# Two weight blocks a group get their low part by an accumulating DMA

## The chip, the cores and the metric

The kernel runs on one core of a Trainium2 chip. The metric is the device time of one execution in microseconds. The core has a matrix engine (TensorE, "PE" in the profile, with its weight loads as "PEld"), VectorE (DVE), ScalarE (ACT), GpSimd (POOL) and SyncE (SP). SP, ACT and POOL can issue DMAs; POOL's go to another queue than SP's.

## What is computed

A trunk of two layers over one sequence of 256 tokens with 2048 features, all in float32: a Conformer convolution layer, then an attention layer, each followed by a gated feed-forward part. The change lies in the two feed-forward parts:

```python
def _swiglu(h, w_gate, w_up, w_down):
    return (jax.nn.silu(h @ w_gate) * (h @ w_up)) @ w_down

h = h + _swiglu(_rmsnorm(h, ffn_norm_g[layer]), ffn_w_gate[layer], ffn_w_up[layer], ffn_w_down[layer])
```

`w_gate` and `w_up` are 2048 x 5632, `w_down` is 5632 x 2048; there is a set of them for each layer.

## The kernel before

**High and low parts.** A product of float32 operands is made from rounded parts (the type F32R). Each operand is split: the high part is the rounded value, the low part is the value less the high part. For a weight block, ACT writes the high part `whi` by a copy that rounds (line 242), and DVE writes the low part `wlo` by a subtraction, raw minus high (line 244). PE then makes three products: activation-high with `whi` (line 420), activation-low with `whi` (line 421), activation-high with `wlo` (line 424). In these products the activation is the operand that PE loads as weights (PEld) and the block of the weight matrix is streamed.

**Blocks.** A weight block is 128 partitions x 1024 float32, 512 KB. SP loads it from DRAM into one of three `raw` buffers (line 294). `whi` and `wlo` have four buffers each. `emit_block` writes out the load and the split of the next block in the list `blocks`; `next_block` sees to it that two blocks beyond the one that PE uses have been written out. A buffer is taken again once its last reader is done: a `raw` buffer after the subtraction that reads it, a `whi` or `wlo` buffer after PE's products with it. `in_order` keeps the splits in their order on ACT and on DVE. Apart from that, a scheduler orders each engine's instructions when the program is built.

**Groups.** Gate and up matrices are worked through in 11 groups of 512 columns for each of the two feed-forward parts (`ffn_hidden`, line 918). Group 0 uses 16 plain blocks. The ten later groups follow the pattern `ITEMS_FF = "nnSnSnSn"`: each `n` stands for one gate block and one up block, and each `S` for a product of 2 x 2 parts that is made with seven multiplications in place of eight. Its sums and differences of weight blocks are made by DVE in `emit_sums` (line 253) from two blocks that POOL loads in `load_sums` (lines 232 and 233); each `S` is four entries in the list. So a later group has 22 entries: ten plain blocks and three `S`. Written as positions, the plain ones are 0 to 3 (two gate blocks, then two up blocks), 8 and 9, 14 and 15, 20 and 21; the `S` entries are 4 to 7, 10 to 13 and 16 to 19. PE uses the entries in this order. Groups alternate between two sets of result banks, called `pp` and `aux`/`b`, for their plain products.

**Between groups.** When a group's products are complete, `combine` and `hidden` (lines 888 to 903) join them, apply SiLU on ACT and multiply on DVE. A few steps into the next group `turned` (line 905) transposes the result on PE, and ACT (line 915) and DVE (line 916) split it into the high and low part of `hid`. This last step frees banks that the first `S` of that group uses.

**The list is made ahead** in `plan_two`, which is called once for each group of gate and up, and for the two halves of `w_down`, with `n_rest` 0 for the former and 3 for the latter:

```python
        ahead = [next(plain) for _ in range(2)]
        blocks.extend((*w, k, GKV) for w in ab for k in ahead)
```

Of the kernel before, what the change touches and what calls it, by code (L numbers as in the profile page):

```python
# [10 lines left out]
F32R = mybir.dt.float32r  # L11
AF = mybir.ActivationFunctionType
ALU = mybir.AluOpType
# [5 lines left out]
S = 256  # L19
# [26 lines left out]


SUMS_FF = 3
LATE = 4
ITEMS_FF = "nnSnSnSn"  # L50

# [41 lines left out]
def trunk(ctx: ExitStack, tc: tile.TileContext, xT, vec, const, w1, w2, wk, wv, wq, wo, wg0, wu0, wd0, wg1, wu1, wd1, fing, out):  # L93
    nc = tc.nc
# [52 lines left out]
    def new_x(pool, name, n=DT):  # L147

        return pool.tile([P, n, 2, S], F32R, name=name)
# [8 lines left out]

    blocks = []
    all_sums = []  # L160

    def plan(w, u, kt_n, gk=GK):
        blocks.extend((w, u, g, gk) for g in range(kt_n // gk))
# [4 lines left out]
    def pairs_of(items, n_sums):  # L168

        n = n_sums if "S" in items else 0  # L170
        return iter(range(n)), iter(range(n, len(items)))

    def plan_two(a, b, items, n_sums, n_rest):

        sums, plain = pairs_of(items, n_sums)
        ab = a, b
        assert items.startswith("nn") and "S" not in items[len(items) - n_rest:]
        ahead = [next(plain) for _ in range(2)]
        blocks.extend((*w, k, GKV) for w in ab for k in ahead)
        for item in items[2:len(items) - n_rest]:  # L180
            if item == "S":
                k = next(sums)
                blocks.extend(("sums", len(all_sums), q, GKV) for q in range(4))
                all_sums.append((a, b, k))
            else:
                k = next(plain)
                blocks.extend((*w, k, GKV) for w in ab)
        rest = list(plain)
        assert len(rest) == n_rest and next(sums, None) is None
        blocks.extend((*w, k, GKV) for w in ab for k in rest)  # L190
# [29 lines left out]
    @contextmanager  # L220
    def in_order(eng):

        with tc.issue_after(last_split[eng]) if eng in last_split else nullcontext():
            made = []
            yield made
        last_split[eng] = made[-1].ins

    def load_sums(n):

        a, b, k = all_sums[n]  # L230
        src = [w[c, k].rearrange("p (k n) -> p k n", k=GKV) for w, c in (a, b)]
        nc.gpsimd.dma_start(places[0][:, 0:4:3, :], src[0])
        nc.gpsimd.dma_start(places[0][:, 1:3, :], src[1])  # L233
# [6 lines left out]
    def split(hi, lo, raw):  # L240
        with in_order("ACT") as made:
            made.append(nc.scalar.copy(hi, raw))  # L242
        with in_order("DVE") as made:
            made.append(nc.vector.tensor_tensor(out=lo, in0=raw, in1=hi.bitcast(F32), op=ALU.subtract))  # L244

    def emit_sums(n, q, _):

        hi, lo = (wp.tile([P, GKV, NBV], F32R, name=n, bufs=AHEAD + 2) for n in ("whi", "wlo"))
        four, t13, t24 = places

        def less(o, a, b):
            with in_order("DVE") as made:
                made.append(nc.vector.tensor_tensor(out=o, in0=a, in1=b, op=ALU.subtract))  # L253

        if q == 0:
            split(hi, lo, four[:, 0:4:3, :])
            less(t13, four[:, 1:3, :], four[:, 0:2, :])
        elif q == 1:
            split(hi[:, 1, :], lo[:, 1, :], four[:, 2, :])
            less(t24[:, 0, :], four[:, 2, :], t13[:, 0, :])  # L260
            less(t24[:, 1, :], four[:, 3, :], t24[:, 0, :])
        elif q == 2:
            split(hi, lo, t13)
        else:
            split(hi, lo, t24)
            if n + 1 < len(all_sums) and all_sums[n + 1][0][0] is all_sums[n][0][0]:
                load_sums(n + 1)
        ready.append((None, hi, lo))

    def emit_block():  # L270
        i = len(ready)
        if blocks[i][0] == "sums":
            emit_sums(*blocks[i][1:])
            return
        w, u, g, gk = blocks[i]
        natural = any(w is a for a in (wg0, wu0, wd0, wg1, wu1, wd1))
        shape = [P, gk, GK * NB // gk]
        native = NATIVE if g == 0 and (w is w1 or w is w2 and u < 2) else 0
        if native:
            raw = conv_pool[0].tile(shape, F32, name="rawn", bufs=2)  # L280
        else:
            raw = wp.tile(shape, F32, name="raw", bufs=RAW)
        hi = lo = None
        if native < gk:
            hi = wp.tile(shape, F32R, name="whi", bufs=AHEAD + 2)
            lo = wp.tile(shape, F32R, name="wlo", bufs=AHEAD + 2)
        src = w[u, g].rearrange("p (k n) -> p k n", k=gk)
        with_x = w is w1 and u == 0
        step = gk if not with_x else 1 if g == 0 else 2
        for s in range(0, gk, step):  # L290
            if with_x:
                load_x(GK * g + s, step)
            part = slice(s, s + step)
            nc.sync.dma_start(raw[:, part, :], src[:, part, :])
            part = slice(max(s, native), s + step)
            if natural:
                split(hi, lo, raw)
                continue
            if part.start < part.stop:
                nc.scalar.copy(hi[:, part, :], raw[:, part, :])  # L300
                eng = nc.gpsimd if (w is w1 and u > 1) or (w is w2 and u < 2 and (u, g) in ((0, 1), (1, 1), (0, 2))) else nc.vector
                eng.tensor_tensor(out=lo[:, part, :], in0=raw[:, part, :], in1=hi[:, part, :].bitcast(F32), op=ALU.subtract)  # L302
        ready.append((raw, hi, lo))
        if with_x and g == DT // GK - 1:
            x_loaded()
# [12 lines left out]
    def later(n, fn):  # L318
        queue.append([n, fn])
# [203 lines left out]
    with tc.tile_pool(name="cv", bufs=1) as cv, tc.tile_pool(name="cvu", bufs=1) as cvu:  # L523
# [11 lines left out]
        def load_x(kt, n):  # L535
            nc.sync.dma_start(hT[:, kt:kt + n, :], xT[:, kt:kt + n, :])
            for j in range(kt, kt + n):
                if j < NATIVE:
                    nc.vector.tensor_scalar(out=xf[:, j, :], in0=hT[:, j, :], scalar1=v("a_g", j), scalar2=None, op0=ALU.mult)
                else:  # L540
                    split_scaled(x, j, v("a_g", j))

        def x_loaded():
            nc.sync.dma_start(cst, const)
            nc.sync.dma_start(vecs[:, 3 * DT:], vec[:, 3 * DT:])
            for j in range(0, DT, 2):
                norm.add(hT[:, j:j + 2, :], *((nc.gpsimd, nc.gpsimd) if j < 4 else (nc.scalar, nc.vector)))
# [138 lines left out]
        for _ in range(3):  # L686
            emit_block()
# [77 lines left out]
    def sum_up(sums, u, two, h, d):  # L765

        h, d = h.rearrange("p (a b) -> p a b", b=S), wide(d)
        two = two.bitcast(F32)
        nc.vector.tensor_tensor(out=h, in0=two[:, :, 0, :], in1=two[:, :, 1, :], op=ALU.add)
        a11, a21, a12, a22 = (h[:, j, t * P:(t + 1) * P] for j in range(2) for t in range(2))  # L770
        for i, a, b, op in ((0, a21, a22, ALU.add), (1, d[:, 0, :], a11, ALU.subtract), (2, a11, a21, ALU.subtract),
                            (3, a12, d[:, 1, :], ALU.subtract)):
            nc.vector.tensor_tensor(out=d[:, i, :], in0=a, in1=b, op=op)
        nc.scalar.copy(sums[:, u, :, 0, :], d)
        nc.vector.tensor_tensor(out=sums[:, u, :, 1, :], in0=d, in1=sums[:, u, :, 0, :].bitcast(F32), op=ALU.subtract)
# [80 lines left out]
    def room(name):  # L856
        return sp.tile([P, 2, S], F32, name=name).rearrange("p a b -> p (a b)")
# [7 lines left out]
    def ffn_hidden(ff, scratch, wg, wu, x, norm):  # L865

        nonlocal hT
        hid = Joined()
        hid.add(new_x(ff, "hid", FT - LATE), FT - LATE)
        rooms = ff.tile([P, 2, 2, NBV], F32, name="rooms", tag="late")  # L870
        sums = ff.tile([P, SUMS_FF, 4, 2, P], F32R, name="xsums", tag="t8")
        later(2, lambda: norm.rstd_nat(bank2))
        for k in range(SUMS_FF):
            later(3 + 3 * k, lambda k=k: sum_up(sums, k, x[:, 2 * k:2 * k + 2, :, :], room("sq"), room("sq")))
# [30 lines left out]
        def turned(c, cs):  # L905

            if c == F // NBV - 1:
                hid.add(ff.tile([P, LATE, 2, S], F32R, name="hid2", tag="late"), LATE)
            for i in range(2):
# [8 lines left out]
        for c in range(F // NBV):  # L918
            items = ff_items(c)
            cs = (second_banks if c % 2 else first_banks)()  # L920
            two_blocks((wg, c), (wu, c), items, SUMS_FF, 0, x, sums, cs, first_banks if c % 2 else second_banks, combine)
            if c == 0:
# [59 lines left out]
    with tc.tile_pool(name="at", bufs=1) as ap:  # L982
# [46 lines left out]
        for c in range(D // NBV):  # L1029
            bk = project_nat(wv, c, x)  # L1030
            for t in range(2):
                nc.scalar.activation(vn[:, t, c * NBV:(c + 1) * NBV], bk[t], AF.Identity,
                                     scale=norm.rn[:, t:t + 1])
# [138 lines left out]
```

## Time and profile before

| | |
|---|---|
| median of 3 runs | 2133.26 us (2132.51 to 2134.04) |
| the profiled execution | 2134.19 us |
| its span, first to last instruction | 2132.4 us |
| clock granted to TensorE | 0.998 of full speed |
| bytes moved by DMA | 410.65 MB |

The span is what the profile's shares are taken of; the execution is 1.8 us longer. In the trace PE passes from one later gate and up group to the next in about 42.6 us; the ten groups lie between 366 and 793 us for the first layer and between 1460 and 1887 us for the second. A plain block is twelve products, which PE begins 0.23 us apart; the duration of one, 0.39 us, is longer since they are pipelined.

In the rows of groups, a line has the source line, the engine, the operation, the tile written and the tiles read, the shapes, the count, and then the busy time in us and the mean of one in ns, and the idle time ahead with what ended it. A row of DMA issues ends with the size of one and the median time in us from issue to landing. A row of waits has who waited for whom, the total in us, the number of times, and the longest. A row of the timeline begins with the start in us from the beginning of the span and the length.

### The profile page before, as it was taken

The numbers are of one execution on the slowest core, as the hardware profiler recorded it, in microseconds if no ns is written. First come the engines' busy times: TensorE is split into PE (matmuls) and PEld (weight loads), VectorE is DVE, ScalarE is ACT, GpSimd is POOL, SyncE is SP. The second block draws the span as 40 slices with busy tenths as digits, with TensorE's granted clock in tenths as the row PEclk, the third lists the DMA queues.
The fourth block names the chain that finished last, engine by engine and source line by source line (L and its number), as shares of the span: only waits on it lengthen the run. The fifth ranks groups of instructions, "written<-read, shape, count | busy, mean of one in ns | idle before, by whom it ended". The sixth has DMA issues, their size and how long they took to land.

```text
span 2132.4 us, 28640 instructions
## 1 busy us (share of the span) xinstructions
PE 2112.3 (99%) x10490; PEld 1789.5 (84%) x10490; DVE 1725.0 (81%) x2323; ACT 1172.0 (55%) x1525; POOL 344.1 (16%) x333
## 2 busy tenths in 40 slices
PE   9999899999999999999999999999999999999998
PEld 8999788888888888888888888888888888888886
DVE  6888876888998898878745677676899899988877
ACT  6665545555555555555644566555555555555454
POOL 5999110000000000000000100011000000000200
PEclk9999999999999999999999999999999999999999
DMA  7555357555655567565665644566556565566664
GB/s 246 185 159 169 97 182 244 177 189 198 213 189 190 199 201 243 192 195 194 193 192 183 189 152 148 174 201 213 198 197 201 194 200 195 198 221 217 210 213 150
DMA packets 114942, 410.65 MB, mean 193 GB/s; under 512 B 12912, under 2 KB 13936, under 8 KB 114800
## 3 DMA queue, kind: packets, MB, share of 16 engines
q1 hardware_dynamic: 87264, 310.21, 45.1%
q0 software_dynamic: 26816, 97.53, 13.1%
q8 instruction: 82, 1.34, 0.2%
q10 hardware_dynamic: 720, 1.07, 0.1%
q14 instruction: 60, 0.49, 0.1%
HBM read 402.47 MB, written 6.29 MB: 192 GB/s over the span
## 4 chain that ended last, share of the span: by engine, by line
PE 96%; DVE 1%; DMA 1%; ACT 0%; issue 0%; POOL 0%; SPq 0%; DVEq 0%; ACTq 0%; POOLq 0%
PE pp L420 12%; PE pp L424 12%; PE pp L421 12%; PE pp L346 10%; PE aux L420 9%; PE aux L424 9%; PE aux L421 9%; PE pp L388 7%; PE pp L350 5%; PE b L420 2%; PE b L421 2%; PE b L424 2%; PE pp L413 1%; DMA raw<-w 1%; PE pp L401 0%; DVE aux L587 0%
## 5 line engine op out<-in xcount | busy, mean ns | idle before, releaser
L244 DVE TENSOR_TENSOR wlo<-raw,whi 128x1024 fp32r<-128x1024 f32 x360 | 431.9, 1230 | 107.1 <-ACT whi L242 93.3
L242 ACT CAST whi<-raw 128x1024 fp32r<-128x1024 f32 x360 | 369.7, 1050 | 250.0 <-DMA raw<-wd 74.7
L300 ACT CAST whi<-raw 128x1024 fp32r<-128x1024 f32 (+1 forms) x209 | 216.1, 1037 | 231.1 <-PE pp L346 93.9
L302 DVE TENSOR_TENSOR wlo<-raw,whi 128x1024 fp32r<-128x1024 f32 (+1 forms) x164 | 201.9, 1243 | 137.8 <-ACT whi L300 116.5
L242 ACT CAST whi<-rooms 128x1024 fp32r<-128x1024 f32 x120 | 126.5, 1055 | 200.4 <-DVE rooms L253 174.2
L420 PE MATMUL pp<-whi,x 128*128 128x512 f32 x522 | 204.7, 392 | 0.0
L421 PE MATMUL pp<-whi,x 128*128 128x512 f32 x522 | 203.2, 389 | 0.0
L420 PE MATMUL aux<-whi,x 128*128 128x512 f32 x414 | 163.7, 395 | 0.0
L421 PE MATMUL aux<-whi,x 128*128 128x512 f32 x414 | 161.3, 390 | 0.0
L233 POOL DMA_DIRECT2D work<-wu x60 | 33.4, 556 | 748.4 <-DVE rooms L253 712.2
L244 DVE TENSOR_TENSOR wlo<-rooms,whi 128x1024 fp32r<-128x1024 f32 x120 | 146.6, 1222 | 8.7 <-ACT whi L242 5.3
L424 PE MATMUL pp<-wlo,x 128*128 128x512 f32 x522 | 150.6, 389 | 0.0
L244 DVE TENSOR_TENSOR wlo<-work,whi 128x1024 fp32r<-128x1024 f32 x120 | 114.4, 954 | 42.3 <-ACT whi L242 41.8
L587 DVE SCALAR_TENSOR_TENSOR aux<-up,vecs,aux 128x256 f32<-128x256 f32 x350 | 140.9, 481 | 1.5 <-ACT aux L585 1.5
L242 ACT CAST whi<-work 128x1024 fp32r<-128x1024 f32 x120 | 95.8, 833 | 77.2 <-DMA work<-wg 42.3
L424 PE MATMUL aux<-wlo,x 128*128 128x512 f32 x414 | 135.1, 390 | 0.0
L420 PE MATMUL pp<-whi,hid 128*128 128x512 f32 x306 | 119.2, 390 | 0.0
L421 PE MATMUL pp<-whi,hid 128*128 128x512 f32 x306 | 119.1, 389 | 0.0
L420 PEld LDWEIGHTS pp<-whi,x 128*128 128x128 f32 x522 | 98.0, 188 | 22.9 <-DVE hid L916 2.9
L424 PEld LDWEIGHTS pp<-wlo,x 128*128 128x128 f32 x522 | 98.0, 188 | 20.6
L421 PEld LDWEIGHTS pp<-whi,x 128*128 128x128 f32 x522 | 98.0, 188 | 20.0
L388 PE MATMUL pp<-x,whi 128*128 128x256 f32 x600 | 111.9, 288 | 0.0
(306 smaller groups left out, 4865.7 us busy)
## 6 DMA issues: line engine op xcount, KB each, us to landing
raw<-wd SPq DMA_DIRECT2D x128, 512.0 KB, 4.2
raw<-wg SPq DMA_DIRECT2D x116, 512.0 KB, 4.0
raw<-wu SPq DMA_DIRECT2D x116, 512.0 KB, 4.0
raw<-w SPq DMA_DIRECT2D x75, 512.0 KB, 3.7
work<-wg POOLq DMA_DIRECT2D x60, 512.0 KB, 4.6
work<-wu POOLq DMA_DIRECT2D x60, 512.0 KB, 3.8
t<-wd POOLq DMA_DIRECT2D x48, 512.0 KB, 4.4
raw<-wv SPq DMA_DIRECT2D x32, 512.0 KB, 4.0
```

What stands on the lines that cost most here:

```text
L233: nc.gpsimd.dma_start(places[0][:, 1:3, :], src[1])
L242: made.append(nc.scalar.copy(hi, raw))
L244: made.append(nc.vector.tensor_tensor(out=lo, in0=raw, in1=hi.bitcast(F32), op=ALU.subtract))
L300: nc.scalar.copy(hi[:, part, :], raw[:, part, :])
L302: eng.tensor_tensor(out=lo[:, part, :], in0=raw[:, part, :], in1=hi[:, part, :].bitcast(F32), op=ALU.subtract)
L346: nc.tensor.matmul(bk[:, m, :, :], hi, x[:, k, :, :], start=k == 0, stop=k == kt_n - 1 and turned, skip_group_check=True)
L350: nc.tensor.matmul(bk[:, m, 0, :], lo, x[:, k, 0, :], start=False, stop=k == kt_n - 1 and not turned, skip_group_check=True)
L388: nc.tensor.matmul(bks[u][:, m, :], a[:, j, m * P:(m + 1) * P], b, start=kt == 0 and m == 0 and i == 0, stop=kt == DT - 1 and i == len(pas ...
L420: nc.tensor.matmul(o, xs[0], hi, start=start, stop=False, skip_group_check=True)
L421: nc.tensor.matmul(o, xs[1], hi, start=False, stop=False, skip_group_check=True)
L424: nc.tensor.matmul(o, xs[0], lo, start=False, stop=stop and last[id(o)] == n, skip_group_check=True)
L587: nc.vector.scalar_tensor_tensor(out=acc[i % 2], in0=win, scalar=w, in1=acc[i % 2], op0=ALU.mult, op1=ALU.add)
```

## The change

In each of the 20 later gate and up groups, the plain blocks at positions 1 and 3 are marked in a set `added`. For a marked block the split is another: ACT writes into `wlo` the raw block times -1, rounded as the high part is, so that `wlo` holds the negated high part. POOL then issues a DMA that reads the block once more from DRAM and adds it onto `wlo` (`accum_op=ALU.add`), which leaves raw minus high there. After that ACT writes `whi` by its copy as before. DVE has no part in these blocks. SP loads the raw block as before.

```diff
+ADDED = 1, 3
...
+    added = set()
...
+        if "S" in items and not n_rest:
+            added.update(len(blocks) + i for i in ADDED)
         blocks.extend((*w, k, GKV) for w in ab for k in ahead)
...
+    def split_added(hi, lo, raw, src):
+        with in_order("ACT") as made:
+            made.append(nc.scalar.activation(lo, raw, AF.Copy, scale=-1.0))
+        nc.gpsimd.dma_start(lo, src.bitcast(F32R), accum_op=ALU.add)
+        with in_order("ACT") as made:
+            made.append(nc.scalar.copy(hi, raw))
...
             nc.sync.dma_start(raw[:, part, :], src[:, part, :])
             part = slice(max(s, native), s + step)
+            if i in added:
+                split_added(hi, lo, raw, src)
+                continue
             if natural:
                 split(hi, lo, raw)
                 continue
```

## The prediction

> **What bounds the kernel now.** The page's first lines come first: which engine fills the span?
>
> ```profile
> span 2132.4 us, 28640 instructions
> PE 2112.3 (99%) x10490; PEld 1789.5 (84%) x10490; DVE 1725.0 (81%) x2323; ACT 1172.0 (55%) x1525; POOL 344.1 (16%) x333
> ```
>
> PE is busy for 2112.3 of 2132.4 us, and the change takes no matmul away. It can gain only where PE waits for a weight block, and lose wherever it makes PE wait. So the stage matters: the busy time by windows, one window per later gate and up group (PE passes one in about 42.6 us).
>
> ```profile
> 451.80:494.40 42.60, 42.13 (x190) 34.64 (x189) 38.75 (x44) 23.41 (x27) 3.81 (x6) 1.00 0.58 198
> 1588.20:1631.00 42.80, 42.80 (x193) 35.01 (x192) 38.74 (x44) 23.55 (x28) 3.81 (x6) 1.00 0.59 197
> ```
>
> The columns are length, PE, PEld, DVE, ACT, POOL, clock, DMA share, GB/s. DVE is 91% busy here (38.75 of 42.60), but PE is without work for 0.47 us in the first window and not at all in the second. What PE does wait for is in the waits view of its weight loads, over the whole span:
>
> ```profile
> PEld aux L420 <- DVE hid L916: 4.2, 10, 0.9
> PEld pp L420 <- DVE hid L916: 2.9, 10, 0.3
> PEld aux L424 <- DVE wlo L244: 0.7, 2, 0.4
> ```
>
> These are all the waits for DVE in the 20 groups: 4.2 + 2.9 + 0.7 = 7.8 us, or 0.37% of the span. That is the ceiling of any gain. Only 0.7 us of it is for a low part; the rest is for L916, the second half of the turned hidden block.
>
> **The change part by part.** Durations and prices:
>
> ```profile
> L244 DVE TENSOR_TENSOR wlo<-raw,whi 128x1024 fp32r<-128x1024 f32 x360 | 431.9, 1230 | 107.1 <-ACT whi L242 93.3 <-PE aux L424 8.2 <-PE pp L424 5.2
> L242 ACT CAST whi<-raw 128x1024 fp32r<-128x1024 f32 x360 | 369.7, 1050 | 250.0 <-DMA raw<-wd 74.7 <-DMA raw<-wg 32.1 <-PE aux L421 32.0
> L242 ACT CAST whi<-work 128x512 fp32r<-128x512 f32 x60 | 37.0, 617 | 12.7 <-ACT whi L242 6.9 <-PE pp L421 3.3 <-issue 2.3
> L900 ACT ACTIVATE work<-work,rstdn 128x512 f32<-128x512 f32 x40 | 26.9, 714 | 0.1
> L232 POOL DMA_DIRECT2D work<-wg x60 | 43.1, 718 | 14.4 <-PE b L421 12.6 <-issue 1.8
> work<-wg POOLq DMA_DIRECT2D x60, 512.0 KB, 4.6
> work<-wu POOLq DMA_DIRECT2D x60, 512.0 KB, 3.8
> hT<-residual POOLq DMA_DIRECT2D x8, 512.0 KB, 8.1
> ```
>
> ADDED names positions 1 and 3 of each later group (the second gate block and the second up block): 2 x 10 groups x 2 feed-forward parts = 40 blocks.
> - Removed: 40 subtractions on DVE, 40 x 1.230 = 49.2 us, 2.46 us a group.
> - Added on ACT: a scaled copy, ahead of the cast. At 512 columns an ACTIVATE takes 714 ns where a cast takes 617, so at 1024 I put 1050 + 97 = 1.15 us; 40 x 1.15 = 46 us, 2.3 us a group on 23.41 of 42.60. Hidden by ACT's idle time; if that cover went, it would cost 46 us.
> - Added on POOL: 40 issues of about 0.72 us, 29 us on an engine that is 16% busy. Each waits for its scaled copy, and POOL's next order, the loads of the sums, stands behind it.
> - Added on the DMA engines: 40 x 0.524 = 21 MB on 410.65.
> - Moved: the raw buffer is now set free by ACT's cast and not by DVE's subtraction, so SP's next load may start up to half a microsecond sooner. That load is not late today.
>
> The new wait is PE's: the low part of an added block is there when the DMA has landed. Is it in time? Four groups in turn, by the timeline: the cast of block 1, which the scaled copy now precedes, and the first use of its low part (L424).
>
> ```profile
> 453.54 1.05 ACT L242 CAST whi<-raw 128x1024 fp32r<-128x1024 f32 x1 [2.56 <-DMA raw<-wg]
> 460.13 0.87 PEld L424 LDWEIGHTS pp<-wlo,x 128*128 128x128 f32 x4
> 496.11 1.05 ACT L242 CAST whi<-raw 128x1024 fp32r<-128x1024 f32 x1 [2.58 <-DMA raw<-wg]
> 503.31 0.87 PEld L424 LDWEIGHTS aux<-wlo,x 128*128 128x128 f32 x4
> 538.97 1.05 ACT L242 CAST whi<-raw 128x1024 fp32r<-128x1024 f32 x1 [2.32 <-DVE work L893]
> 546.05 1.07 PE L424 MATMUL pp<-wlo,x 128*128 128x512 f32 x4
> 581.53 1.05 ACT L242 CAST whi<-raw 128x1024 fp32r<-128x1024 f32 x1 [2.63 <-DMA raw<-wg]
> 588.84 1.07 PE L424 MATMUL aux<-wlo,x 128*128 128x512 f32 x4
> ```
>
> The weight load runs 0.23 us ahead of its matmul, so the spans are 6.59, 7.20, 6.85 and 7.08 us. Less 1.15 for the scaled copy and 0.06 for the hand-over (an estimate), the DMA has 5.4, 6.0, 5.6 and 5.9 us: about 5.5 in groups that sum in pp, 5.9 in the others. Today a subtraction of 1.23 us stands there with over 4 us to spare. The copy cannot start sooner: ACT waits for raw<-wg.
>
> How long does the DMA take? No row shows an accumulating one. The bounds: 3.8 us, the plain 512 KB load by POOL, below; 8.1 us, the slowest 512 KB row of POOL, above. An addition must read two blocks of 512 KB, so the nearest rows are the two loads that POOL issues as a pair, 0.56 us apart: the second lands 0.56 + 4.6 = 5.2 us after the first is issued. That alone would just fit.
>
> But the DMA engines are not free at that time:
>
> ```profile
> 456.13 0.33 SPq L294 DMA_DIRECT2D raw<-wg  x1
> 458.00:459.00 1.00, 1.00 (x7) 0.81 (x6) 0.49 (x1) 1.00 (x2) 0.00 (x0) 1.00 0.96 389
> 459.00:460.00 1.00, 1.00 (x6) 0.84 (x5) 0.66 (x1) 1.00 (x3) 0.00 (x0) 1.00 0.07 25
> 460.00:461.00 1.00, 1.00 (x6) 0.84 (x5) 1.00 (x3) 1.00 (x2) 0.00 (x0) 1.00 0.00 0
> 470.00:471.00 1.00, 1.00 (x6) 0.80 (x5) 1.00 (x2) 1.00 (x3) 0.00 (x0) 1.00 1.03 422
> ```
>
> SP's next load (issued at 456.13, about where the accumulation starts after 454.75) takes 0.524 MB / 0.4 = 1.3 us of the engines. Shared between the queues, it puts the accumulation back by between 0 and 1.3 us; I take 1.0, since the transfers overlap wholly. So 5.2 + 1.0 = 6.2 us against 5.5 and 5.9: PE waits 0.7 us in ten groups and 0.3 in ten, together 10 us. The wait comes again in each group, because the cast of block 1 follows from PE's own progress (buffers that PE frees, then the loads). With 5.2 the sum is nothing; with 8.1, 10 x 2.6 + 10 x 2.2 = 48 us.
>
> The Trainium skill, "Collectives: The Full Stack", section "The bandwidth ceiling: the fold count and why AG ≠ RS ≠ AR", says that an add in the DMA engine needs two source reads, so that a reducing transfer runs at half the rate of a copy. No run here shows it yet; as an estimate it makes of the 3.8 us row 3.8 + 1.3 = 5.1 us, and 6.1 with the sharing (waits of 10 x 0.6 + 10 x 0.2 = 8 us), where the plain row and the same sharing, 4.8 us, would let the change be hidden.
>
> Block 3 has more room:
>
> ```profile
> 457.63 1.05 ACT L242 CAST whi<-raw 128x1024 fp32r<-128x1024 f32 x1 [0.87 <-DMA raw<-wu]
> 465.80 1.07 PE L424 MATMUL pp<-wlo,x 128*128 128x512 f32 x4
> 467.04 0.56 POOL L233 DMA_DIRECT2D work<-wu  x1 [19.47 <-DVE rooms L253]
> ```
>
> From 457.63 + 1.21 to 465.57 are 6.7 us, at a time when the DMA engines stand still (0.07 and 0.00 above). It costs nothing up to 6.7 us, and POOL has been idle for 19 us before it must issue the sums' loads at 467.04.
>
> What does DVE's relief bring? The wait for L916 is at the first sum of the group:
>
> ```profile
> 468.29 2.00 ACT L242 CAST whi<-raw 128x1024 fp32r<-128x1024 f32 x2
> 470.19 0.57 ACT L915 CAST hid<-aux 128x512 fp32r<-128x512 f32 x1
> 469.56 2.35 DVE L244 TENSOR_TENSOR wlo<-raw,whi 128x1024 fp32r<-128x1024 f32 x2
> 471.83 0.68 DVE L916 TENSOR_TENSOR hid<-aux,hid 128x512 fp32r<-128x512 f32 x1
> 472.57 0.19 PEld L420 LDWEIGHTS aux<-whi,xsums 128*128 128x128 f32 x1 [0.91 <-DVE hid L916]
> 511.25 1.05 ACT L242 CAST whi<-raw 128x1024 fp32r<-128x1024 f32 x1 [0.99 <-PE aux L421]
> ```
>
> L916 stands behind two subtractions of plain blocks that are not added, and these start 0.2 us after their cast can be done (468.29 + 1.05 = 469.34, against 469.56). ACT, held by PE, sets the pace here and not DVE: in the other kind of group the cast itself waits for PE (511.25). An earlier DVE moves L916 by 0.2 us at most: 10 x 0.15 = 1.5 us of gain, out of 7.8.
>
> Sum: +10.0 - 1.5 = +8.5 us on the profiled execution (2134.19, span 2132.4). That run is 0.9 above the median of 2133.26, which the forecast starts from: 2133.26 + 8.5 = 2141.8.
>
> **The rivals.**
> - The DMA is in time, at 5.5 us or less: no wait is added, and 0 to 4 us of L916 go: 2129.5 to 2133.3. For it: the 3.8 us row and the pair's 5.2; against it: the engines' share of 0.96. The same holds up to waits of 4 us in all. This ends on the other side of the forecast, not slower; it decides at a landing of 5.5 us after the copy's end.
> - The addition is slow, near the 8.1 us row: PE waits over 2 us a group for block 1, and block 3 with its 6.7 us is no cover any more: +48, 2181. For it: no row excludes it; against it: the 8.1 us row reads back from DRAM among other loads.
> - DVE's relief does more than I see, as the scheduler finds another order once DVE is free: all 7.8 us of waits go, 2125.5. For it: DVE at 91%; against it: L916 is paced by PE and ACT.
> - The change does not do what it says, if the accumulation is issued late because POOL is held by another order. POOL is idle for 19 us before 467.04, so this has little for it.
>
> **How the numbers follow.** 0.2% (4.3 us) is about what a measurement of this kernel can tell from no change. Forecast (waits of 0.3 to 1 us a group, 2138 to 2155): 0.37. Slow addition (above 2155): 0.16. In time: 0.36. More relief (under 2129): 0.11. So slower 0.53, same 0.36, faster 0.11. The range goes from 2130, a hidden DMA with most of L916's gain, to 2181 by the 8.1 us bound; left out are 0.11 below and some 0.05 above.
>
> **What would show it.** In the changed kernel's waits, PEld at L424 should wait for a DMA on wlo about 20 times, by 0.3 to 0.8 us, and the DMA view should give the new issue near 6 us to landing. DVE should fall by 49 us, ACT rise by 46, POOL's issues grow by 40. If the landing is under 5.4 us, the middle rival holds; if L916's waits shrink by more than 2 us, I have misread what holds that step; if PE waits at block 3 too, the addition is slower than any row here.

## The result and the profile after

The kernel with the change takes 2186.46 us (median of 4 runs, 2183.82 to 2190.64) against 2133.16 us (4 runs, 2132.51 to 2134.04) beside it: 1.0251 times as long, with an interval from 1.0234 to 1.0269. That is 53.3 us more. The forecast had the sign, and 8.5 us.

In the changed kernel line numbers are shifted: L244 is now L248, L242 is L246, L420, L421 and L424 are L434, L435 and L438, L294 is L305, L916 is L930. New are L252 (the scaled copy), L253 (the adding DMA) and L255 (the cast of an added block).

The first lines of the page after:

```profile
span 2184.8 us, 28755 instructions
PE 2127.3 (97%) x10490; PEld 1792.7 (82%) x10490; DVE 1683.9 (77%) x2283; ACT 1206.3 (55%) x1565; POOL 380.0 (17%) x373
```

DVE has lost 41.1 us of work (49 were forecast), ACT has gained 34.3 (46 forecast) and POOL 35.9 (29 forecast), and the span is 52.4 us longer: relief for an engine that was not the bound, paid for on the one that was. What PE's weight loads wait for, in total, times and longest:

```profile
PEld pp L438 <- DMA wlo<-wg: 22.6, 10, 3.8
PEld aux L438 <- DMA wlo<-wg: 21.5, 10, 2.9
...
PEld aux L434 <- DVE hid L930: 3.0, 10, 0.3
PEld pp L434 <- DVE hid L930: 2.9, 10, 0.3
PEld pp L438 <- DMA wlo<-wu: 2.3, 5, 0.8
...
PEld aux L438 <- DMA wlo<-wu: 1.2, 3, 0.6
```

The new wait is where the forecast put it and four times its size: `wlo<-wg` is block 1, 22.6 + 21.5 = 44.1 us, 2.2 us in each of 20 groups; `wlo<-wu`, block 3, adds 3.5. Together 47.6 us. The waits for L930 went from 7.1 to 5.9. So 47.6 - 1.2 = 46.4 of the 52.4 us are these waits; 6.0 are left over, of which more below.

The DMA view after (tile, queue, count, size, median from issue to landing), beginning with the line of POOL's queue (packets, MB, share of 16 engines' span):

```profile
q0 software_dynamic: 32576, 118.50, 18.2%
...
wlo<-wg POOLq DMA_DIRECT2D x20, 512.0 KB, 7.2
wlo<-wu POOLq DMA_DIRECT2D x20, 512.0 KB, 8.2
```

And the same queue before:

```profile
q0 software_dynamic: 26816, 97.53, 13.1%
```

Block 1 lands after 7.2 us where 6.2 were forecast. The queue's line also has the price of the addition in engine time: before, 13.1% of 2132.4 us for 97.53 MB is 279.3 us, or 1.50 us for a block of 0.524 MB. After, 18.2% of 2184.8 is 397.6 us. The 118.3 us more, over 40 added blocks, are 2.96 us each, 1.97 times the mean block of before. The kernel with plain DMAs at the same places (below) is the closer comparison: 16.6% of 2142.3 us is 355.6, or 76.3 more than before, so a plain block there takes 1.91 us, and the addition 1.55 times that. The rule that the prediction named beside its sum (the Trainium skill, "Collectives: The Full Stack", section "The bandwidth ceiling: the fold count and why AG ≠ RS ≠ AR": an adding transfer reads two sources and so runs at half the rate) asks for 2, and the traces give 1.55 to 1.97, according to what the plain block is.

One group on the timeline after, with the lines of ACT, POOL, SP and PE that matter (start, length, and in brackets the idle time and its releaser):

```profile
456.59 1.06 ACT L252 ACTIVATE wlo<-raw 128x1024 fp32r<-128x1024 f32 x1 [2.65 <-DMA raw<-wg]
...
457.95 0.90 POOL L253 DMA_DIRECT2D wlo<-wg  x1 [7.41 <-DVE work L907]
...
458.62 0.33 SPq L305 DMA_DIRECT2D raw<-wg  x1
...
461.32 0.33 SPq L305 DMA_DIRECT2D raw<-wu  x1
...
465.15 1.20 PE L438 MATMUL pp<-wlo,x 128*128 128x512 f32 x4 [1.64 <-DMA wlo<-wg]
```

The copy ends at 457.65 and POOL issues at 457.95: a hand-over of 0.30 us where the forecast put 0.06. The engine that the bracket names, DVE at L907, had long been done; it was ACT's copy. SP issues one load 0.67 us behind the addition and a second 3.4 us behind it. The landing is at 465.1, 7.1 us after the issue; SP's first load lands 0.2 us after that and the second another 1.1 us later. PE's weight load had been waiting for 2.06 us by then, so it was wanted 5.1 us after the issue.

### The profile page after: what moved, and what is told of

It reads as the page before. It is cut to its first block, busy times and chain, and to the rows that moved or that the text cites. A ratio compares the mean times of both kernels' runs of the same rounds, so it can differ in the third digit from the quotient of the medians.

```text
span 2184.8 us, 28755 instructions
## 1 busy us (share of the span) xinstructions
PE 2127.3 (97%) x10490; PEld 1792.7 (82%) x10490; DVE 1683.9 (77%) x2283; ACT 1206.3 (55%) x1565; POOL 380.0 (17%) x373
## 3 DMA queue, kind: packets, MB, share of 16 engines
q0 software_dynamic: 32576, 118.50, 18.2%
## 4 chain that ended last, share of the span: by engine, by line
PE 66%; DMA 13%; issue 9%; DVE 8%; ACT 2%; POOL 1%; SPq 0%; POOLq 0%; DVEq 0%; ACTq 0%
PE pp L360 10%; PE pp L438 7%; PE pp L434 7%; PE pp L435 7%; PE pp L402 7%; DMA wlo<-wg 6%; PE pp L364 5%; PE aux L438 5%; PE aux L434 5%; PE aux L435 5%; DMA work<-wg 3%; DVE rooms L264 3%; DVE wlo L248 2%; DMA wlo<-wu 2%; ACT whi L246 2%
## 5 line engine op out<-in xcount | busy, mean ns | idle before, releaser
L248 DVE TENSOR_TENSOR wlo<-raw,whi 128x1024 fp32r<-128x1024 f32 x320 | 384.8, 1232 | 136.6 <-ACT whi L246 117.1
L246 ACT CAST whi<-raw 128x1024 fp32r<-128x1024 f32 x320 | 327.5, 1049 | 189.4 <-DMA raw<-wd 85.5
L246 ACT CAST whi<-rooms 128x1024 fp32r<-128x1024 f32 x120 | 126.4, 1053 | 234.3 <-DVE rooms L264 107.0
L434 PE MATMUL pp<-whi,x 128*128 128x512 f32 x522 | 206.7, 396 | 0.0
L435 PE MATMUL pp<-whi,x 128*128 128x512 f32 x522 | 205.0, 393 | 0.0
L248 DVE TENSOR_TENSOR wlo<-rooms,whi 128x1024 fp32r<-128x1024 f32 x120 | 146.7, 1223 | 57.9 <-ACT whi L246 45.8
L438 PE MATMUL pp<-wlo,x 128*128 128x512 f32 x522 | 153.7, 395 | 19.0 <-DMA wlo<-wg 18.3
L434 PE MATMUL aux<-whi,x 128*128 128x512 f32 x414 | 164.6, 398 | 0.0
L248 DVE TENSOR_TENSOR wlo<-work,whi 128x1024 fp32r<-128x1024 f32 x120 | 114.7, 956 | 62.3 <-ACT whi L246 49.5
L435 PE MATMUL aux<-whi,x 128*128 128x512 f32 x414 | 162.5, 392 | 0.0
L438 PE MATMUL aux<-wlo,x 128*128 128x512 f32 x414 | 137.9, 397 | 17.4 <-DMA wlo<-wg 17.2
L438 PEld LDWEIGHTS pp<-wlo,x 128*128 128x128 f32 x522 | 97.6, 189 | 44.7 <-DMA wlo<-wg 22.6
L246 ACT CAST whi<-work 128x1024 fp32r<-128x1024 f32 x120 | 94.5, 832 | 67.2 <-DMA work<-wg 33.5
L434 PE MATMUL pp<-whi,hid 128*128 128x512 f32 x306 | 119.2, 390 | 0.0
L435 PE MATMUL pp<-whi,hid 128*128 128x512 f32 x306 | 119.1, 389 | 0.0
L434 PEld LDWEIGHTS pp<-whi,x 128*128 128x128 f32 x522 | 99.1, 190 | 23.4 <-DVE hid L930 2.9
L435 PEld LDWEIGHTS pp<-whi,x 128*128 128x128 f32 x522 | 99.2, 190 | 20.6
```

The source lines that it names most:

```text
L434: nc.tensor.matmul(o, xs[0], hi, start=start, stop=False, skip_group_check=True)
L435: nc.tensor.matmul(o, xs[1], hi, start=False, stop=False, skip_group_check=True)
L438: nc.tensor.matmul(o, xs[0], lo, start=False, stop=stop and last[id(o)] == n, skip_group_check=True)
```

## The experiments

Three questions were open. Is the landing long because the addition is slow, or because other loads run beside it? Does the place of the block matter, or only its room? Is DVE's relief worth nothing, or is it hidden behind the new wait? Kernels that were timed have a ratio to the kernel before, run beside them on the same chip.

**A plain DMA in place of the adding one.** The low part of the 40 blocks is then the raw block: the adding of the negated high part is left out.

```diff
-        nc.gpsimd.dma_start(lo, src.bitcast(F32R), accum_op=ALU.add)
+        nc.gpsimd.dma_start(lo, src.bitcast(F32R))
```

> The DMA onto the low part stays where it is but does not add: the low part of the 40 blocks becomes the raw block, so the computation is changed there. Scaled copy, POOL's issue and the bytes read from DRAM stay. Theory A (the addition makes the DMA long: 2.96 us of all 16 engines each, from the queue's share, against 1.50 for a plain POOL load): the landing falls from a median of 7.2 and 8.2 to 4 to 5 us, which is under the 5.5 us that block 1 has, PE's waits for it go from 47.6 us to under 5, and the time comes back to 2131 to 2138. Theory B (one more 512 KB among the other loads at that moment is late, added or not): the landing stays above 6 us and the time above 2150.

2144.35 us, 1.0044 (1.0029 to 1.0059). Its DMA view:

```profile
wlo<-wg POOLq DMA_DIRECT2D x20, 512.0 KB, 5.2
wlo<-wu POOLq DMA_DIRECT2D x20, 512.0 KB, 6.5
```

Its waits:

```profile
PEld pp L438 <- DMA wlo<-wg: 6.8, 5, 1.7
...
PEld aux L438 <- DMA wlo<-wg: 1.9, 3, 1.1
```

At the same place a plain block lands after 5.2 us and the adding one after 7.2. These are medians of 20, and those of the plain one spread, from 3.7 to 6.9 us in the later groups but the first of each layer. The addition costs 2.0 us there; everything else that the change does (copies, issues, 21 MB more, and what a plain block is late) costs 9 us in all. So most of the loss goes with the addition, though neither expectation held: the landings and the time lie between the two. But 5.2 is also 1.4 more than the 3.8 us in which POOL's faster loads of a plain block land: the place costs too.

**One of the two positions alone.**

```diff
-ADDED = 1, 3
+ADDED = 1,
```

> Only position 1 is marked. If PE's wait is set by the landing at position 1 alone, 44 of the 53 us stay: 2175 to 2182, with a landing of about 7.2 us. If the second accumulating DMA crowds the first, the landing falls towards 6 and the time to 2140 to 2160.

```diff
-ADDED = 1, 3
+ADDED = 3,
```

> Only position 3 is marked: 20 accumulating DMAs, none at position 1. In the trace of after PE waited 44.1 us at position 1 and 3.5 us at position 3. If position 3 has the room that the prediction counted (6.7 us and more), the time is 2132 to 2138. If the accumulating DMA takes 7 us or more with no other beside it, its landing here is still 7.0 or more and PE waits up to 0.5 us in some groups: 2133 to 2140. If the 7 to 8 us come from the two accumulating DMAs and the loads crowding each other, the landing falls below 6.5.

Position 1 alone: 2175.06 us, 1.0189 (1.0161 to 1.0216), waits of 22.8 + 18.6 = 41.4 us in the profiled execution (2181.12, the slowest of four), nearly all of the change's 44.1. Its landing is 7.2 us as with both, so it is not the second addition that makes the first one late. Position 3 alone: 2150.38 us, 1.0075 (1.0058 to 1.0091). So "it costs nothing" of the forecast does not hold for block 3: with both added it is covered by PE's wait for block 1 (where PE waits for it, its need comes 7.5 to 8.5 us after the issue; alone, 5.4 to 6.1, but for a layer's first group), and alone it shows. The wait in the run with position 3 alone:

```profile
PEld pp L438 <- DMA wlo<-wu: 17.2, 9, 2.4
```

And its timeline in a group that sums in `pp`, ACT, POOL and SP:

```profile
460.29 0.72 ACT L914 ACTIVATE work<-work,rstdn 128x512 f32<-128x512 f32 x1 [0.23 <-DVE work L913]
460.92 1.04 ACT L252 ACTIVATE wlo<-raw 128x1024 fp32r<-128x1024 f32 x1
...
462.26 0.90 POOL L253 DMA_DIRECT2D wlo<-wu  x1 [12.33 <-ACT wlo L252]
...
462.71 0.33 SPq L305 DMA_DIRECT2D raw<-wu  x1
463.13 0.38 SPq L305 DMA_DIRECT2D raw<-wg  x1
```

The forecast took its room from the cast of before, at 457.63 in its group. Here the scaled copy stands behind the two SiLU activations of L914 (460.92), and two of SP's loads are issued within 0.9 us of the addition: its stretch no longer has the idle DMA engines that the trace of before had. The landing here is 7.6 us. In the groups that sum in `aux` SP's two loads come 1.1 us and more behind the addition; there it lands after 5.3 to 5.8 us and PE does not wait.

**Position 0 in place of 1.** The first gate block has more room than the second; if only room counted, it should be better.

```diff
-ADDED = 1, 3
+ADDED = 0, 3
```

> Marked are positions 0 and 3 in place of 1 and 3: the same number of accumulating DMAs, the same relief of DVE. In the trace of before the cast of block 0 lies 8.3 to 8.6 us ahead of the first use of its low part, where block 1 has 6.6 to 7.2; less 1.06 for the scaled copy and 0.30 for the hand-over that is 7.0 to 7.2 us of room. If room against landing is what decides, the waits at wlo<-wg fall from 44 us to under 15 (landing 7 to 8 us) and the time to 2140 to 2165, those of position 3 staying. If an accumulating DMA costs the same wherever it stands (by its traffic, or by the clock), the time stays at 2180 to 2190.

2243.88 us, 1.0506 (1.0483 to 1.0528): twice as bad. Its DMA view for that block, and then its timeline:

```profile
wlo<-wg POOLq DMA_DIRECT2D x20, 512.0 KB, 9.1
```

```profile
462.80 0.33 SPq L305 DMA_DIRECT2D raw<-wg  x1
...
463.61 0.90 POOL L253 DMA_DIRECT2D wlo<-wg  x1 [3.30 <-ACT wlo L252]
...
463.94 0.81 SPq L305 DMA_DIRECT2D raw<-wu  x2
```

There the addition is issued among three of SP's loads, and the landing goes from 7.2 to 9.1. The room is larger than block 1's, 6.6 to 6.8 us in most groups, and yet PE waits longer, 28.4 + 23.6 = 52.0 us where it waited 44.1: room alone is not the measure. The larger part of the growth is at block 3, which is marked as before:

```profile
PEld pp L438 <- DMA wlo<-wu: 20.1, 8, 3.6
...
PEld aux L438 <- DMA wlo<-wu: 16.1, 9, 3.0
```

It had 3.5 us behind an added block 1; here, behind one at position 0, it has 36.2. All waits for an added `wlo` come to 88.2 us, the longest 6.0.

**The block read from the raw buffer in place of DRAM.**

```diff
-        nc.gpsimd.dma_start(lo, src.bitcast(F32R), accum_op=ALU.add)
+        nc.gpsimd.dma_start(lo, raw.bitcast(F32R), accum_op=ALU.add)
```

> The accumulating DMA reads the raw block from its buffer in SBUF, not from DRAM again. The raw buffer is then held until the DMA has landed, so SP's next load is not beside it. If crowding by that load is a large part of the 7.2 us (second_only had landings down to 5.3), the landing at position 1 falls to 5 to 6 us; the held buffer may then make a later block late instead. If the addition alone takes 7 us, nothing falls: landing 7 or more and time at 2180 or above.

2157.02 us, 1.0099 (1.0085 to 1.0112). The waits are 11.4 + 10.8 = 22.2 us, half of the change's, and the landings have a median of 6.6 us (4.4 to 8.9); but the two places part here. Sorted by place, block 1 lands after 4.7 us and makes PE wait 3.6 us in all; block 3 lands after 7.1 and makes it wait 18.6, about as much as in the run with position 3 alone. So the loss at block 1 is nearly gone. Two things changed there at once: the source, and SP's next load, which waits for the held raw buffer and comes 2.5 us or more behind the addition and not 0.7. This run does not divide the 2.5 us between them.

**Half a block by DMA, half by DVE.**

```diff
-            made.append(nc.scalar.activation(lo, raw, AF.Copy, scale=-1.0))
-        nc.gpsimd.dma_start(lo, src.bitcast(F32R), accum_op=ALU.add)
+            made.append(nc.scalar.activation(lo[:, 0, :], raw[:, 0, :], AF.Copy, scale=-1.0))
+        nc.gpsimd.dma_start(lo[:, 0, :], src[:, 0, :].bitcast(F32R), accum_op=ALU.add)
...
+        with in_order("DVE") as made:
+            made.append(nc.vector.tensor_tensor(out=lo[:, 1, :], in0=raw[:, 1, :], in1=hi[:, 1, :].bitcast(F32), op=ALU.subtract))
```

> Positions 1 and 3 as in after, but only the first half of each block's low part (512 of 1024 columns) comes by the accumulating DMA; DVE subtracts the other half. If the landing is made of bytes (2.96 us of all engines for a whole block), it falls by about 1.5 us, to 5.5 to 6 us at position 1, and the room grows by 0.4 us: waits of 0 to 0.5 us a group, 2135 to 2150. If it is mostly a fixed latency of an adding DMA, the landing stays above 6.5 and the time above 2155.

2135.55 us, 1.0000 (0.9991 to 1.0009). Its busy times, and then its waits for L932 (L930 of the change):

```profile
PE 2113.4 (99%) x10490; PEld 1788.8 (84%) x10490; DVE 1704.5 (80%) x2323; ACT 1191.8 (56%) x1565; POOL 380.1 (18%) x373
```

```profile
PEld aux L436 <- DVE hid L932: 3.4, 10, 0.7
...
PEld pp L436 <- DVE hid L932: 2.9, 10, 0.3
```

The half lands after 4.8 and 4.2 us (5.5 to 6 were expected) and is hidden but for 1.7 us in all. DVE does 20.5 us less work than before, and the time does not move: 0.8 us of L916's waits go. This is the cleanest measure of what DVE's relief is worth here: nothing that can be told from no change.

**The landing by itself.** Behind the last output of the kernel before, a chain that measures POOL's load of one block seven ways, four times each; the time of the whole tells nothing. `negated` is the scaled copy of ACT into a fresh `wlo`, `raw_after` a copy of ACT into a `raw` buffer, so that the next step waits for the one ahead.

```diff
+            lo = negated(a)
+            nc.gpsimd.dma_start(lo, src.bitcast(F32R))
+            lo = negated(lo.bitcast(F32))
+            nc.gpsimd.dma_start(lo, src.bitcast(F32R), accum_op=ALU.add)
+            raw, = raw_after(lo, 1)
+            lo = negated(raw)
+            nc.sync.dma_start(raw, s1)
+            nc.gpsimd.dma_start(lo, src.bitcast(F32R), accum_op=ALU.add)
...
```

> The kernel before, with a chain added behind its last output: four times in turn, POOL's load of 512 KB plain with nothing beside it; adding with nothing beside it; adding beside one load of SP; adding beside two; plain beside two; adding 256 KB alone; adding 512 KB out of SBUF alone. ACT writes the tile anew between the steps, so each waits for the one ahead. It measures landings, and the time of the whole tells nothing. Theory (the landing of 7.2 us is 3.8 of a plain load, about 2.0 for the addition and about 1.4 for the loads beside it): plain alone 3.7 to 4.0, adding alone 5.4 to 6.0, beside one load 6.2 to 7.0, beside two 7.0 to 8.3, plain beside two about 1.5 less than that, half alone 3.7 to 4.2. Rival (the adding transfer is slow in itself, 7.0 us at the least whatever runs beside it): adding alone 6.8 to 7.2, beside loads hardly more, half alone 4.5 and more.

The view of each line in turn (plain alone, adding alone, adding beside one load of SP, adding beside two, plain beside two, half alone, out of SBUF alone) ends with this:

```profile
DMA to landing us min/median/max: 3.8/3.8/3.8
...
DMA to landing us min/median/max: 5.5/5.6/5.7
...
DMA to landing us min/median/max: 6.3/6.4/6.5
...
DMA to landing us min/median/max: 6.5/7.4/7.9
...
DMA to landing us min/median/max: 5.0/5.5/6.7
...
DMA to landing us min/median/max: 4.0/4.1/4.2
...
DMA to landing us min/median/max: 4.4/4.4/4.5
```

This settles the first question. The addition by itself costs 5.6 - 3.8 = 1.8 us, of which 0.31 is a longer issue on POOL (0.87 against 0.56 us). One load beside it costs 0.8 more, a second 1.0 more, and a plain load suffers the same from two (5.5 - 3.8 = 1.7). The rival, an addition of 7 us whatever runs beside it, is out. So is a fixed price per transfer: half a block saves 1.5 of 5.6 us.

The chain's loads are issued ahead of the addition (0.27 us, the other 1.23), where the kernel's comes 0.67 us behind it, so its prices for a load don't carry over as they stand. Two other traces say which load it is that makes 7.2 us of 5.6. With position 3 alone, in the groups that sum in `aux`, two loads issued 1.1 us and more behind the addition cost nothing (5.3 to 5.8 us). At position 9 (next), in the same kind of group, SP issues one load 0.7 us behind it and no other until the landing, and nine of the ten additions take 7.1 to 7.4 us. So the one load that follows closely is enough for the 1.6 us; the second, 3.4 us behind, isn't needed for it.

**Another place, ahead of L916.** Position 9 is the second of the two plain blocks whose subtractions stand ahead of L916 on DVE.

```diff
-ADDED = 1, 3
+ADDED = 9,
```

> Only the block at position 9 of each of the 20 groups gets its low part by the adding DMA, positions 1 and 3 are split as before. In the trace of before its room is about 6.6 us (cast at 469.34, low part loaded at 477.46, less 1.06 and 0.30 and the wait of 0.2 of its first product), as much as any place has, and the DMA engines are in use until 475.2 by loads of SP and POOL. It is also the second of the two subtractions ahead of L916. Theory (the place decides by what shares the engines): landing 8 to 9 us, PE waits 1.4 to 2.4 us a group, 2160 to 2185 us, and L916 brings nothing back, since ACT's L915 moves back by 1.06 us. Rival (the addition takes 7.0 to 7.2 wherever it stands): waits of 0.3 to 0.6 us a group, 2138 to 2148. Rival (DVE's relief is worth something where it stands ahead of L916): some 4 us less than either.

2193.92 us, 1.0278 (1.0264 to 1.0292): with half as many added blocks, slower than the change itself, and outside what each theory gave. Its waits:

```profile
PEld aux L438 <- DMA wlo<-wu: 39.2, 10, 4.1
...
PEld pp L438 <- DMA wlo<-wu: 5.3, 10, 1.5
...
PEld pp L434 <- DVE hid L930: 3.0, 10, 0.3
PEld aux L434 <- DVE hid L930: 2.9, 10, 0.3
```

Its landing, and its timeline in a group that sums in `aux`, ACT, POOL and SP:

```profile
DMA to landing us min/median/max: 6.4/7.0/8.0
```

```profile
519.86 1.06 ACT L252 ACTIVATE wlo<-raw 128x1024 fp32r<-128x1024 f32 x1 [1.94 <-PE pp L438]
...
521.22 0.90 POOL L253 DMA_DIRECT2D wlo<-wu  x1 [6.36 <-ACT wlo L252]
...
521.88 0.33 SPq L305 DMA_DIRECT2D raw<-wg  x1
...
532.87 0.33 SPq L305 DMA_DIRECT2D raw<-wu  x1
```

The expectation failed in two ways. The landing was 7.0 and not 8 to 9, as the rival said. And the room of 6.6 us was read from one kind of group: in the ten groups that sum in `pp` the waits are 0.5 us, as that room gives. In the ten others the scaled copy must wait for PE to free the `wlo` buffer (the bracket: 1.94 us for PE at L438), and the waits are 3.9 us. The addition of this group lands at 528.3 and had been wanted 3.7 us earlier, 3.4 us after its issue: half the room. The prediction had looked at both kinds of group for position 1; here only one was looked at. L930's waits are 5.9 us as with the change, so relief right ahead of L916 brings no more than relief elsewhere.

> The same place, but only the first half of the block by the adding DMA (256 KB), the other half by DVE. Theory: landing 4 to 5.5 us, hidden by the room of 6.6 us; DVE is 0.6 us earlier at L916 in the groups that wait for it by up to 0.9, ACT's L915 is 0.6 us later: between no change and 4 us less, 2131 to 2136. Rival (crowding makes even the half late): waits of PE for wlo from a DMA, over 2138.

The same place with the half-block edit: 2138.82 us, 1.0019 (1.0010 to 1.0028). The half lands after 5.6 us and makes PE wait 4.8 us, 2.9 of them once; L932's waits go from 7.1 to 6.2. So it went as the rival of the expectation had it, and again there is no gain.

**The subtraction on POOL, without a DMA.** To take DVE's work away without the new transfer:

```diff
-            made.append(nc.scalar.activation(lo, raw, AF.Copy, scale=-1.0))
-        nc.gpsimd.dma_start(lo, src.bitcast(F32R), accum_op=ALU.add)
-        with in_order("ACT") as made:
             made.append(nc.scalar.copy(hi, raw))
+        nc.gpsimd.tensor_tensor(out=lo, in0=raw, in1=hi.bitcast(F32), op=ALU.subtract)
```

> The blocks at positions 1 and 3 get their low part by a subtraction on POOL in place of the DMA: the same 49 us are taken off DVE, with no accumulating DMA. A subtraction of this size took POOL 2.4 us in the first stage, well within the 5.5 us. If DVE's relief is worth next to nothing, as the prediction argued (L916 is paced by PE and ACT): 2130 to 2134, with PE's waits for L916 near their 7.1 us. If the relief is worth all the waits: 2125 to 2127.

> No DMA: the block at position 8 alone gets its low part by a subtraction on POOL (2.4 us). Its subtraction on DVE stands ahead of L916 (the second half of the turned hidden block), which PE waits for by 7.1 us in all. If DVE's order there is what holds L916, the waits shrink by 2 to 6 us: 2127 to 2132 beside a before of 2133. If L916 is paced by PE and ACT, as the prediction said: 2132 to 2135, no difference.

At positions 1 and 3 it takes 2135.39 us, 1.0002 (0.9992 to 1.0011); but it is a poor measure of relief. DVE is busy for 1714.4 us, only 10.6 less than before, though 49.2 us of subtractions left it. At position 8 alone (with `ADDED = 8,`) it takes 2148.42 us, 1.0059 (1.0047 to 1.0072), and the wait and the timeline show why:

```profile
PEld aux L432 <- DVE hid L928: 17.4, 10, 1.8
```

```profile
469.78 2.40 POOL L253 TENSOR_TENSOR wlo<-raw,whi 128x1024 fp32r<-128x1024 f32 x1 [1.31 <-PE pp L436]
470.62 2.65 DVE L248 TENSOR_TENSOR wlo<-raw,whi 128x1024 fp32r<-128x1024 f32 x1 [0.82 <-ACT whi L246]
```

DVE's next subtraction takes 2.65 us beside POOL's, where it takes 1.22 elsewhere, and L928 (L916 of before) comes later than if DVE had done both. The wait for it goes from 4.2 to 17.4 us in that kind of group. Neither time that was expected came, since the edit slowed DVE where it was to relieve it.

## Where the last 6 us went

The waits leave 6.0 of the 52.4 us unexplained, and the run's mean clock is 0.992 against 0.998. The changed kernel in windows around its longest wait (length, PE, PEld, DVE, ACT, POOL, clock, DMA share, GB/s):

```profile
1771.00:1772.00 1.00, 1.00 (x4) 0.81 (x3) 0.11 (x1) 0.00 (x0) 0.00 (x0) 0.50 0.99 258
...
1775.00:1776.00 1.00, 1.00 (x4) 0.80 (x3) 0.00 (x0) 0.06 (x1) 0.65 (x1) 0.50 0.08 4
1776.00:1777.00 1.00, 1.00 (x6) 0.76 (x5) 0.00 (x0) 0.99 (x1) 0.00 (x0) 0.99 0.73 246
```

The weight load that ended the wait:

```profile
1770.37 1.36 PEld L438 LDWEIGHTS pp<-wlo,x 128*128 128x128 f32 x4 [3.83 <-DMA wlo<-wg]
```

After a wait of 3.83 us PE works at half its clock until 1776: four matmuls a microsecond where there are six later. Each dip of this kind in the traces lasts 3.4 or 6.8 us and begins within 1.5 us of the wait's end. The busy share shows none of it; the count in brackets does.

For each run the clock that was not granted was added up, over 186 windows of 10 us from 260 to 2120 us, as (1 - clock) x 10. It is set beside the part of the span's growth that the waits don't explain: span less 2132.4, less the waits for an added `wlo`, plus what went of L916's 7.1 us.

| run | waits for wlo | longest | left of the span | clock not granted |
|---|---|---|---|---|
| the change | 47.6 | 3.8 | 6.0 | 10.2 |
| position 1 alone | 41.4 | 4.4 | 6.7 | 8.5 |
| positions 0 and 3 | 88.2 | 6.0 | 20.3 | 23.9 |
| position 9 | 44.5 | 4.1 | 16.3 | 22.2 |
| half at position 9 | 4.8 | 2.9 | 1.7 | 1.7 |
| position 3 alone | 17.2 | 2.4 | -0.1 | 0 |
| from the raw buffer | 22.2 | 2.0 | -1.2 | 0 |
| plain DMA | 12.8 | 1.7 | -1.7 | 0 |

For the change the third number is 52.4 - 47.6 + 1.2 = 6.0. The last two columns go together, and they go with the longest wait and not with the sum: the three runs whose waits stay at 2.4 us or below lose no clock, though one of them waits for 22.2 us in all, and each run with a wait of 2.9 us or more does. In the half at position 9, one wait of 2.93 us, at 1789, is followed by the only dip in that stretch. In the changed kernel the dips follow waits of 2.39, 2.50, 2.86, 2.88 and 3.83 us; waits of 2.42, 2.54 and 2.59 us go without. Length alone does not decide: at position 9 one of ten waits of 3.7 to 4.1 us has no dip, and with positions 0 and 3 one dip, at 1797, follows two waits of 0.98 and 1.15 us close together. The cause is read from this order and this table; no kernel was run that kept PE busy through a long wait. The Trainium skill, "TensorE: Matmul & The Clock Gate", section "HAM oscillation — how this bites in real kernels", gives as rule no PE-idle gaps over about 3.4 us. Its half rate is what the rows show; its limit is not: here waits from 2.4 us on can cost it, and the measurement decides.

## Why the prediction was wrong

- **PE bounds, and the ceiling of any gain is 7.8 us**: right. Of 49.2 us taken off DVE 1.2 came back, at L916, where 1.5 were forecast, and the half-block kernel, almost without the new wait, shows no gain (1.0000).
- **The wait goes to PE at the low part of block 1**: right, in every one of the 20 groups. The mechanism of the forecast is the one that decided.
- **The landing of 6.2 us**: this step failed. It was made of 5.2, for a block that reads two sources, plus 1.0 for SP's next load. The median was 7.2; the mean of the 20 additions of block 1 is 7.5, since the first group of each layer takes 10.5 and 9.7. Both terms were too small: measured by itself the addition is 5.6, and the one load that was counted costs 1.6 us (7.2 - 5.6) and not 1.0. That is above even the 1.3 us that the prediction took as the most. It depends on when the load is issued: nothing at 1.1 us and more behind the addition, 1.6 at 0.7 behind. Why 0.4 us more or less decides so much stays open.
- **The room of 5.4 to 6.0 us**: too long for the change. PE's need came 5.1 us after the issue in the group at 458 above, and 5.1 again in the group after it (issue at 502.59, weight load at 509.94 after a wait of 2.28). Leaving out the first group of each layer, which has 8.1 us, the rooms run from 3.5 to 5.8, with a median of 5.1 in both kinds of group, where 5.5 and 5.9 were forecast. With position 1 alone the medians are 5.5 and 5.6: for that the forecast was nearly right, though the hand-over from ACT to POOL takes 0.30 us and not 0.06, of which the scaled copy gives 0.09 back (1.06 us where 1.15 were forecast). The rest is missing only where block 3 is added too; how that shortens the room stays open.
- Together: the mean wait of 2.2 us is a landing of 7.5 less a room of 5.3, where 6.2 less 5.7 were forecast. The wait was the small difference of two times of some six microseconds, one of them taken from rows 4.3 us apart (3.8 and 8.1), so an error of a fifth in the landing became one of four times in the wait.
- **Block 3 costs nothing**: wrong, though it cost little here (3.5 us). Its landing of 8.2 us is above the 8.1 us of POOL's slowest 512 KB row before, as the prediction said of a wait at block 3. Alone it costs 15 us (2150.38 against 2135.29 beside it). Its room was read from the order of before, and the copy was placed behind the SiLU.
- **The clock**: left out. It is the likely cause of the last 6 us and the reason that the time, 2186, lies above even the upper bound of the range, whose waits (48 us, by the rival "slow addition") nearly match the measured 47.6 and which has nothing behind them.

The rival "slow addition" described the result best: over 2 us a group for block 1, and 48 us. It was right in size by luck and not in its ground: its 48 us are a landing of 8.1 less rooms of 5.5 and 5.9, where means of 7.5 and 5.3 were measured, while the addition by itself is 5.6 us, near the 5.2 that was taken, and the load beside it brought it to 7.2. The prediction weighed the addition and its surroundings as if only one of them could be worse than the nearest row.

## What to carry to other kernels

Work taken off an engine that is not the bound is worth the waits that name it and no more, 7.8 us here, however busy it is; read those first, and then ask what the replacement's own delay does at the point of use. Where a forecast is the small difference between a landing and a room, take both from the whole surroundings: look at each load that shares the engines until the landing and at when it is issued, and read the room in each kind of group, with the order that the edit will make. The addition of a 512 KB block landed after 5.3 to 9.6 us here, according to its neighbours (a layer's first group apart), so it fits only where the room is above that, or for half a block.

## What the hardware showed that was not expected

- An adding DMA of 512 KB takes 2.96 us of all engines against 1.91 for a plain one at the same places (1.50 for the mean block of before), its issue on POOL 0.87 to 0.90 us against 0.56, and its landing alone is 5.6 us against 3.8. Out of the on-chip memory it is 4.4, of half the size 4.1.
- One load of SP issued 0.7 us behind the addition brings its landing from 5.6 to 7.2 us; two that are issued 1.1 us and more behind leave it at 5.3 to 5.8.
- Waits of PE of 2.4 us and more were often, not always, followed by 3.4 or 6.8 us at half clock. The three runs of the table whose longest wait is 2.4 us or less lost nothing, so the cost of a wait is not proportional: position 9, with waits of 3.9 us in ten groups, lost 16 us on top of them.
- A subtraction on DVE that stands beside one on POOL takes 2.65 us in place of 1.22.
- From the end of ACT's copy to POOL's issue that waits for it pass 0.30 us.
